# A fused decoder layer on one core: masks, score banks, compressed product and gates of its attention

## The chip, the cores and the metric

One core of a Trainium2 chip runs the whole layer as one program. The time is device microseconds of one execution; the kernel before takes 1240.49 us, the median of three runs (1238.05 to 1242.54). One more execution was profiled, and all rows below come from it.

## The reference, cut to what matters

The layer takes 512 tokens of width 1024. Two token mixers run side by side on the normalised input: a gated linear recurrence (HGRN2, 8 heads) and a sparse attention with 16 query heads in 4 groups, each group sharing one key/value head of width 64. Their outputs are gated, projected, added to the input; a squared-ReLU MLP and a per-layer embedding follow.

The attention has three branches, each a masked softmax, added with per-head gates:

```python
s = einsum('bgrqd,bgnd->bgrqn', qb, k_cmp)                    # compressed keys, 31 of them
p_cmp = masked_softmax(s, cmp_end <= t_pos); o_cmp = p_cmp @ v_cmp
s = einsum('bgrqd,bgqkd->bgrqk', qr, kg)                      # selected blocks
o_sel = masked_softmax(s, key_pos <= t_pos) @ vg
s = einsum('bgrqd,bgkd->bgrqk', qr, kwb)                      # sliding window of 512
o_win = masked_softmax(s, causal and in window) @ vwb
out = gt[0] * o_cmp + gt[1] * o_sel + gt[2] * o_win           # gt: sigmoid gates per head
```

With 512 tokens there are 8 blocks and 16 may be selected, so every earlier block is chosen; the window also covers all of the past. Both the second and the third branch are therefore plain causal softmax attention with keys of their own.

## The kernel before, in words

Values are kept as pairs of fp32r tiles (a rounded high part and the rest as low part), and a product is the sum of two or three matmuls over the pairs. Projections (`job_n`, L125, and `job_t`, L118 with `mm3`, L81) take 256 or 512 columns per matmul. ScalarE casts the high part and VectorE or GpSimd subtracts for the low part (`split`, L59).

The attention part is `attend` (L454), called once per group of four heads. It is a generator that walks over four tiles of 128 queries (t) and two branches (br). For each (t, br), `scores` (L457) handles the group's four heads one after another. A head takes a bank of the score buffer (two banks, tag `sc`), multiplies its query tile with the high and the low keys (L463, L464; the keys seen are nk = 128, 256, 384 or 512 for t = 0 to 3), and adds the causal mask to the last 128 columns as a third matmul, identity times mask, both in bf16 (L465). VectorE takes the row maximum, negated, from the bank (L467); ScalarE computes the exponential from the bank into a tile P and the row sum beside it (L469). After four heads VectorE inverts the sums (L472) and multiplies them with the branch's gates (L474); three of the P tiles are scaled by the result on VectorE (L477), the fourth on ScalarE (L479). The loop starts the scores of the next (t, br) before `values` (L482) of the present one: for each block of 128 keys the four P tiles are transposed (L158) into a bank, split into `pth` (ScalarE) and `ptl` (VectorE), and multiplied with the values into the bank `py` (L489, L490).

The compressed branch is computed for the group beforehand. `cmp_probs` (L440) leaves its weights, already gated, transposed in `chl`: rows 0 to 63 hold the high and low parts of an even tile t, rows 64 to 127 those of the odd tile after it. After branch 1 of a tile, L517 multiplies the tile's 64 rows with the compressed values `vch` (filled in `cmp_out`, L315 to L317, the same values in all four groups of 32 rows) into `py`, and `store` (L492) evacuates it.

The order of instructions in each engine's queue is chosen by a planner that schedules the program by modelled times. Projections of later stages are fillers: `mark` (L67) notes the mask matmuls and some others with weights, and `spread` (L70) ties the starts of projections to these marks, in proportion. GpSimd does the low parts of weights during attention (`lo_eng`), the rotations and small scalings. The tile `vch` and the constant masks are allocated at the start (L213 to L228).

Of the kernel before, what the change touches and what calls it, by code (L numbers as in the profile page):

```python
# [7 lines left out]
FT = mybir.dt.float32  # L8
FR = mybir.dt.float32r
# [19 lines left out]
def hybrid_layer(ctx: ExitStack, tc: tile.TileContext, x, p, w_in, w_branch_a, w_branch_b, w_out,  # L29
# [21 lines left out]

    ident = const.tile([128, 128], FT, name="ident")
    identr = const.tile([128, 128], FR, name="identr")
    identb = const.tile([128, 128], BF, name="identb")
    half = const.tile([128, 4], FT, name="half")
    dve.memset(half, -0.5)

# [110 lines left out]
    with tc.tile_pool(name="pre", reuse_waits="tile", bufs=2) as pre, \  # L168
            tc.tile_pool(name="prep", reuse_waits="tile", bufs=2, space=PSUM) as prep:
        xs = [pre.tile([128, D], FT, name="xt", bufs=4) for _ in range(NT)]  # L170
        wrow = pre.tile([1, D], FT, name="wrow", bufs=1)
        ones = pre.tile([1, 128], FT, name="ones", bufs=1)
        dve.memset(ones, 1.0)
        sp.dma_start(xs[0], x[0:128])
        act.dma_start(wrow, norm_pre_mix)
        act.dma_start(ident, c_ident)
        first_chunks = n_chunks(w_in, [(C_KS, 128), (C_VS, 128)])
        for t in range(1, NT):
            sp.dma_start(xs[t], x[t * 128:(t + 1) * 128])
        act.copy(identr, ident)  # L180
        dve.tensor_copy(identb, ident)
        wps = prep.tile([128, D], FT, name="wps", bufs=1)
        for i in range(2):
            pe.matmul(wps[:, i * 512:i * 512 + 512], ones, wrow[:, i * 512:i * 512 + 512],
                      start=True, stop=True)
        for t in range(NT):
            sq = pre.tile([128, D], FT, name="sq")
            ss = pre.tile([128, 1], FT, name="ss")
            rs = pre.tile([128, 1], FT, name="rs")
            act.activation(sq, xs[t], AF.Square, accum_out=ss)  # L190
            rstd(rs, ss, EPS, pre)
            un = pre.tile([128, D], FT, name="un")
            for g in range(2):
                c = slice(g * 512, g * 512 + 512)
                dve.scalar_tensor_tensor(un[:, c], xs[t][:, c], rs, wps[:, c], op0=OP.mult, op1=OP.mult)
                ps = transpose4(prep, [un[:, (4 * g + i) * 128:(4 * g + i + 1) * 128] for i in range(4)])
                s = (slice(None), slice(4 * g, 4 * g + 4), slice(t * 128, t * 128 + 128))
                split(uh[s], ul[s], ps.rearrange("p (k t) -> p k t", k=4))
# [14 lines left out]
    ns_keep = tc.alloc_tile_pool(name="nsk", reuse_waits="tile", bufs=1, side="right")  # L213
    bd = ns_keep.tile([128, 4, 64], FT, name="bd")
    pool.memset(bd, 0.0)
    vch = ns_keep.tile([128, 4, 128], FR, name="vch")
    gate = ns_keep.tile([128, NT, 48], FT, name="gate")
    cmask = ns_keep.tile([128, NT, 32], FT, name="cmask")
    sp.dma_start(cmask, c_cmask.rearrange("(t p) n -> p t n", p=128))
# [2 lines left out]
    dve.tensor_scalar(valid[:, 0:1], cmask[:, 0, 0:1], 0.0, None, op0=OP.is_equal)  # L222
    rope = ns_keep.tile([128, NT, 32], FT, name="rope")
    sp.dma_start(rope, c_rope.rearrange("(t p) n -> p t n", p=128))
    causal = ns_keep.tile([128, 128], BF, name="causal")
    cf = ns_keep.tile([128, 128], FT, name="cf")
    sp.dma_start(cf, c_causal)
    dve.tensor_copy(causal, cf)  # L228
# [53 lines left out]
    def cmp_out(b, ph):  # L282
# [25 lines left out]
        else:  # L308
# [4 lines left out]
            vc = cp.tile([32, 4, 64], FT, name="vc")  # L313
            act.activation(vc, po[:32, :256].rearrange("p (g d) -> p g d", g=4), AF.Copy, scale=0.5)
            for r in range(0, 128, 32):  # L315
                act.copy(vch[r:r + 32, :, 0:64], vc)
                dve.tensor_sub(vch[r:r + 32, :, 64:128], vc, vch[0:32, :, 0:64])  # L317


    ns = tc.alloc_tile_pool(name="ns", reuse_waits="tile", bufs=2, side="right")  # L320
# [133 lines left out]
    def attend(g, qs, chl, kvs):  # L454
        P2, j = divmod(g, 2)

        def scores(t, br):  # L457
            KH, KL, V = kvs[br]
            q, nk = slice(t * 128, t * 128 + 128), (t + 1) * 128
            Ps, sums = [], at.tile([128, 4], FT, name="sums", bufs=4)  # L460
            for h in range(4):
                ps = nsp.tile([128, 512], FT, name="ps_s", tag="sc")
                pe.matmul(ps[:, :nk], qs[h][:, q], KH[j][:, :nk], start=True, stop=False)  # L463
                pe.matmul(ps[:, :nk], qs[h][:, q], KL[j][:, :nk], start=False, stop=False)  # L464
                mark(pe.matmul(ps[:, nk - 128:nk], identb, causal, start=False, stop=True), nk / 512)  # L465
                nm = at.tile([128, 1], FT, name="nm", bufs=6)
                dve.tensor_reduce(nm, ps[:, :nk], axis=AX.X, op=OP.max, negate=True)  # L467
                pt = at.tile([128, 512], FT, name="P", bufs=8)
                act.activation(pt[:, :nk], ps[:, :nk], AF.Exp, bias=nm, accum_out=sums[:, h:h + 1])  # L469
                Ps.append(pt)  # L470
            r = at.tile([128, 4], FT, name="r", bufs=4)
            dve.reciprocal(r, sums)  # L472
            gi = 16 * (br + 1) + 4 * g
            dve.tensor_mul(r, r, gate[:, t, gi:gi + 4])  # L474
            for h in range(4):
                if h < 3:
                    dve.tensor_scalar(Ps[h][:, :nk], Ps[h][:, :nk], r[:, h:h + 1], None, op0=OP.mult)  # L477
                else:
                    act.activation(Ps[h][:, :nk], Ps[h][:, :nk], AF.Copy, scale=r[:, h:h + 1])  # L479
            return Ps  # L480
# [28 lines left out]
        for i, (t, br) in enumerate(steps):  # L509
# [3 lines left out]
            values(t, br, pend, py)  # L513
            pend = nxt
            if br:
                o = t % 2 * 64
                pe.matmul(py, vch[o:o + 64, g], chl[t // 2][o:o + 64], start=False, stop=True)  # L517
                store(t, py)
            yield True

# [707 lines left out]
```

## Time and profile before

| | |
|---|---|
| median of three runs | 1240.49 us (1238.05 to 1242.54) |
| profiled execution | 1240.57 us, span 1238.8 us from the first to the last instruction |
| TensorE busy | 1195.2 us (96%), 7199 matmuls |
| VectorE, ScalarE, GpSimd busy | 794.4, 629.3, 169.3 us |
| mean granted TensorE clock | 0.996 of full speed |
| attention stage | from about 129 to 411 us |

Times in rows are microseconds unless marked ns. L465 is line 465 of the kernel. PE is TensorE's matmuls, PEld its weight loads, DVE VectorE, ACT ScalarE, POOL GpSimd. [...]

### The profile page before, as it was taken

How to read it: one execution, taken by the hardware profiler on the slowest of the kernel's cores; microseconds unless marked ns; L12 is line 12 of the kernel's file. 1: busy time of each engine (PE TensorE's matmuls, PEld its weight loads, DVE VectorE, ACT ScalarE, POOL GpSimd, SP SyncE). 2: the span in 40 equal slices, each digit the busy share in tenths (PEclk: the TensorE clock that was granted, in tenths of full speed). 3: DMA queues.
4: the chain of work that ended last, by engine and by line, in shares of the span. 5: the costliest groups of instructions: out<-in, count | busy, mean ns of one | idle time of the engine just before them, and what ended most of it. 6: DMA issues, size and time to landing. Idle time of an engine off the chain costs nothing.

```text
span 1238.8 us, 18866 instructions
## 1 busy us (share of the span) xinstructions
PE 1195.2 (96%) x7199; PEld 1029.5 (83%) x7199; DVE 794.4 (64%) x1448; ACT 629.3 (51%) x1273; POOL 169.3 (14%) x281
## 2 busy tenths in 40 slices
PE   7999999999999999999999999997999999999997
PEld 6888877787777889898978778887989889889885
DVE  6775687847787366767685454587527547555664
ACT  6555677756777433434443222465627437336442
POOL 2022332342321110101010110100000000000000
PEclk9999999999999999999999999999999999999999
DMA  6336222212112432222223994533413424226401
GB/s 180 104 107 167 64 54 54 52 52 61 50 40 74 137 102 69 69 69 69 69 69 103 238 232 151 182 132 113 137 49 106 133 68 137 85 69 225 166 18 68
DMA packets 131597, 127.63 MB, mean 103 GB/s; under 512 B 8578, under 2 KB 107826, under 8 KB 131507
## 3 DMA queue, kind: packets, MB, share of 16 engines
q1 hardware_dynamic: 121504, 109.59, 30.2%
q0 software_dynamic: 3200, 10.49, 3.1%
q10 hardware_dynamic: 6802, 6.36, 1.6%
q8 instruction: 56, 0.92, 0.3%
q14 instruction: 35, 0.28, 0.1%
HBM read 111.73 MB, written 14.68 MB: 102 GB/s over the span
## 4 chain that ended last, share of the span: by engine, by line
PE 83%; DVE 7%; DMA 4%; ACT 4%; issue 1%; SPq 0%; POOL 0%; ACTq 0%; DVEq 0%; POOLq 0%
PE up L1033 11%; PE ps L82 7%; PE ps L83 7%; PE ps L84 7%; PE acc L1116 5%; PE acc L1115 5%; PE acc L1117 5%; PE ps L133 5%; PE ps L135 4%; PE ps L134 4%; PE lev L711 3%; PE tr L158 3%; PE acc L915 2%; PE acc L917 2%; PE acc L916 2%; PE tr L1033 2%
## 5 line engine op out<-in xcount | busy, mean ns | idle before, releaser
L60 ACT CAST whi<-raw 128x1024 fp32r<-128x1024 f32 (+1 forms) x199 | 207.4, 1046 | 219.9 <-PE acc L1117 59.1
L61 DVE TENSOR_TENSOR wlo<-raw,whi 128x1024 fp32r<-128x1024 f32 (+1 forms) x181 | 220.8, 1224 | 124.9 <-ACT whi L60 120.1
L133 PE MATMUL ps<-whi,uh 128*128 128x256 f32 (+1 forms) x512 | 148.0, 290 | 1.4 <-DVE kcd L257 0.5
L135 PE MATMUL ps<-whi,ul 128*128 128x256 f32 (+1 forms) x512 | 146.6, 287 | 0.0
L134 PE MATMUL ps<-wlo,uh 128*128 128x256 f32 (+1 forms) x512 | 146.3, 286 | 0.2 <-DVE wlo L61 0.2
L82 PE MATMUL ps<-uh,whi 128*128 128x512 f32 x288 | 118.2, 411 | 0.0
L84 PE MATMUL ps<-uh,wlo 128*128 128x512 f32 x288 | 114.7, 398 | 0.3 <-DVE wlo L61 0.3
L83 PE MATMUL ps<-ul,whi 128*128 128x512 f32 x288 | 114.7, 398 | 0.0
L1116 PE MATMUL acc<-wlo,fh 128*128 128x512 f32 x256 | 101.0, 395 | 0.0
L1115 PE MATMUL acc<-whi,fh 128*128 128x512 f32 x256 | 100.3, 395 | 0.0
L133 PEld LDWEIGHTS ps<-whi,uh 128*128 128x128 f32 x512 | 96.7, 189 | 4.0 <-PE cps L84 0.7
L1117 PE MATMUL acc<-whi,fl 128*128 128x512 f32 x256 | 99.9, 395 | 0.0
L134 PEld LDWEIGHTS ps<-wlo,uh 128*128 128x128 f32 x512 | 96.9, 189 | 1.3 <-DVE wlo L61 0.5
L135 PEld LDWEIGHTS ps<-whi,ul 128*128 128x128 f32 x512 | 96.7, 189 | 0.6 <-issue 0.2
L469 ACT ACTIVATE P<-ps_s,nm 128x128 f32<-128x128 f32 (+3 forms) x128 | 67.7, 530 | 28.3 <-DVE nm L467 25.9
L467 DVE TENSOR_REDUCE nm<-ps_s 128x1 f32<-128x128 f32 (+3 forms) x128 | 61.2, 484 | 26.4 <-PE ps_s L465 25.8
L61 DVE TENSOR_TENSOR ptl<-tr,pth 128x512 fp32r<-128x512 f32 x82 | 55.5, 684 | 26.5 <-ACT pth L60 26.2
L84 PEld LDWEIGHTS ps<-uh,wlo 128*128 128x128 f32 x288 | 54.1, 188 | 12.6 <-DVE wlo L61 0.4
L83 PEld LDWEIGHTS ps<-ul,whi 128*128 128x128 f32 x288 | 54.2, 188 | 10.2
L82 PEld LDWEIGHTS ps<-uh,whi 128*128 128x128 f32 x288 | 54.2, 188 | 10.0
L1033 PE MATMUL up<-mgh,whi 128*128 128x256 f32 x192 | 54.5, 285 | 3.6 <-ACT mgh L60 3.6
L1117 PEld LDWEIGHTS acc<-whi,fl 128*128 128x128 f32 x256 | 48.2, 188 | 11.2
(323 smaller groups left out, 2942.8 us busy)
## 6 DMA issues: line engine op xcount, KB each, us to landing
raw<-in_w_in_dram SPq DMA_DIRECT2D x58, 512.0 KB, 3.8
raw<-in_w_up_dram SPq DMA_DIRECT2D x32, 512.0 KB, 3.8
raw<-in_w_down_dram SPq DMA_DIRECT2D x32, 512.0 KB, 4.0
raw<-in_w_in_dram SPq DMA_DIRECT2D x17, 256.0 KB, 3.5
raw<-in_w_branch_a_dram SPq DMA_DIRECT2D x8, 512.0 KB, 7.9
raw<-in_w_branch_b_dram SPq DMA_DIRECT2D x32, 128.0 KB, 6.4
raw<-in_w_out_dram SPq DMA_DIRECT2D x8, 512.0 KB, 4.8
raw<-in_w_ple_gate_dram SPq DMA_DIRECT2D x8, 512.0 KB, 5.2
```

The lines of the kernel that those rows point to most:

```text
L60: act.copy(hi, src)
L61: (lo_eng or dve).tensor_sub(lo, src, hi)
L82: rec.append(pe.matmul(ps, lh, rh, start=first, stop=False).ins)
L83: pe.matmul(ps, lh, rl, start=False, stop=False)
L84: pe.matmul(ps, ll, rh, start=False, stop=last)
L133: rec.append(pe.matmul(o, stat[0][:, k, s], hi[:, i], start=(k == 0), stop=False).ins)
L134: pe.matmul(o, stat[0][:, k, s], lo[:, i], start=False, stop=False)
L135: pe.matmul(o, stat[1][:, k, s], hi[:, i], start=False, stop=(k == NK - 1))
L1033: pe.matmul(ps[:, c], l[:, k, cs], r[:, k], start=f and n == 0, stop=e and n == 2, skip_group_check=True)
L1115: pe.matmul(ps, fh[:, k % 4, s], hi[:, k % 2], start=(k == 0), stop=False)
L1116: pe.matmul(ps, fh[:, k % 4, s], lo[:, k % 2], start=False, stop=False)
L1117: pe.matmul(ps, fl[:, k % 4, s], hi[:, k % 2], start=False, stop=(k == NK - 1))
```

## The change

The mask and its identity become fp32r, and the bf16 identity goes. In `scores`, as many heads as fit 512 columns share a bank: four at nk = 128, two at 256, one at 384 and 512. The score matmuls of these heads write their own columns of the bank, one mask matmul then covers the last 128 columns of each head (the same mask, repeated), and one maximum over the bank gives a column per head. The exponentials stay one per head. The compressed values get two copies, one with zeros in rows 64 to 127 and one with zeros in rows 0 to 63, and L517 becomes a product over all 128 rows with the copy that fits the tile's parity. The tile is cleared on GpSimd first. The gates are no longer multiplied into the inverted sums of four heads: the scaling of a P tile on VectorE takes the gate as its second scalar, and the fourth head's factor is multiplied by itself, for ScalarE.

```diff
-    identb = const.tile([128, 128], BF, name="identb")
-        dve.tensor_copy(identb, ident)
-    vch = ns_keep.tile([128, 4, 128], FR, name="vch")
+    vch = ns_keep.tile([128, 2, 4, 128], FR, name="vch")
+    pool.memset(vch.bitcast(FT), 0.0)
-    causal = ns_keep.tile([128, 128], BF, name="causal")
+    causal = ns_keep.tile([128, 128], FR, name="causal")
             for r in range(0, 128, 32):
-                act.copy(vch[r:r + 32, :, 0:64], vc)
-                dve.tensor_sub(vch[r:r + 32, :, 64:128], vc, vch[0:32, :, 0:64])
+                o = r // 64
+                act.copy(vch[r:r + 32, o, :, 0:64], vc)
+                dve.tensor_sub(vch[r:r + 32, o, :, 64:128], vc, vch[0:32, 0, :, 0:64])
...
-            for h in range(4):
-                ps = nsp.tile([128, 512], FT, name="ps_s", tag="sc")
-                pe.matmul(ps[:, :nk], qs[h][:, q], KH[j][:, :nk], start=True, stop=False)
-                pe.matmul(ps[:, :nk], qs[h][:, q], KL[j][:, :nk], start=False, stop=False)
-                mark(pe.matmul(ps[:, nk - 128:nk], identb, causal, start=False, stop=True), nk / 512)
-                nm = at.tile([128, 1], FT, name="nm", bufs=6)
-                dve.tensor_reduce(nm, ps[:, :nk], axis=AX.X, op=OP.max, negate=True)
-                pt = at.tile([128, 512], FT, name="P", bufs=8)
-                act.activation(pt[:, :nk], ps[:, :nk], AF.Exp, bias=nm, accum_out=sums[:, h:h + 1])
-                Ps.append(pt)
+            nm = at.tile([128, 4], FT, name="nm", bufs=3)
+
+            n = max(1, 512 // nk)
+            for h0 in range(0, 4, n):
+                bank = nsp.tile([128, 512], FT, name="ps_s", tag="sc")
+                ps = bank[:, :n * nk].rearrange("p (h k) -> p h k", h=n)
+                for i in range(n):
+                    for K in (KH, KL):
+                        pe.matmul(ps[:, i], qs[h0 + i][:, q], K[j][:, :nk], start=(i == 0 and K is KH),
+                                  stop=False, skip_group_check=True)
+                mark(pe.matmul(ps[:, :, nk - 128:nk], identr, causal[:, None, :].to_broadcast([128, n, 128]),
+                               start=False, stop=True, skip_group_check=True), n * nk / 512)
+                dve.tensor_reduce(nm[:, h0:h0 + n], ps, axis=AX.X, op=OP.max, negate=True)
+                for i in range(n):
+                    h = h0 + i
+                    pt = at.tile([128, 512], FT, name="P", bufs=8)
+                    act.activation(pt[:, :nk], ps[:, i], AF.Exp, bias=nm[:, h:h + 1],
+                                   accum_out=sums[:, h:h + 1])
+                    Ps.append(pt)
...
-            dve.tensor_mul(r, r, gate[:, t, gi:gi + 4])
+            gs = gate[:, t, gi:gi + 4]
+            dve.tensor_scalar(r[:, 3:4], r[:, 3:4], gs[:, 3:4], None, op0=OP.mult)
             for h in range(4):
                 if h < 3:
-                    dve.tensor_scalar(Ps[h][:, :nk], Ps[h][:, :nk], r[:, h:h + 1], None, op0=OP.mult)
+                    dve.tensor_scalar(Ps[h][:, :nk], Ps[h][:, :nk], r[:, h:h + 1], gs[:, h:h + 1],
+                                      op0=OP.mult, op1=OP.mult)
...
-                o = t % 2 * 64
-                pe.matmul(py, vch[o:o + 64, g], chl[t // 2][o:o + 64], start=False, stop=True)
+                pe.matmul(py, vch[:, t % 2, g], chl[t // 2], start=False, stop=True)
```

## Rows read from the trace of the kernel before

**Rows 1.** Chain that ended last: share of the span by engine.
```profile
PE 83%; DVE 7%; DMA 4%; ACT 4%; issue 1%; SPq 0%; POOL 0%; ACTq 0%; DVEq 0%; POOLq 0%
```

**Rows 2.** Windows: length, busy PE, PEld, DVE, ACT, POOL, clock, DMA share, GB/s.
```profile
129.00:411.00 282.00, 266.60 (x1709) 213.34 (x1707) 210.52 (x474) 199.79 (x514) 86.78 (x120) 0.99 0.20 53
205.00:209.00 4.00, 2.28 (x13) 1.57 (x13) 3.82 (x13) 2.54 (x10) 2.65 (x3) 0.98 0.23 50
```

**Rows 3.** Waits of PE in attention: who for whom, total us, times, longest.
```profile
PE ps_s L463 <- ACT P L469: 5.8, 12, 0.9
```

**Rows 4.** Waits of PEld in attention, the compressed product's weight loads.
```profile
PEld py L517 <- issue: 4.0, 16, 0.4
```

**Rows 5.** Timeline of PE around one compressed product: start, us, instruction.
```profile
181.39 0.46 PE L490 MATMUL py<-ptl,V 128*128 128x512 f32 x1
181.78 0.50 PE L517 MATMUL py<-chl,vch 64*128 64x512 f32 x1
182.21 0.66 PE L158 MATMUL tr<-ident,P 128*128 128x128 f32 x4
```

**Rows 6.** Timeline of PE, 512-column projections without a wait.
```profile
410.12 0.39 PE L83 MATMUL ps<-ul,whi 128*128 128x512 f32 x1
410.35 0.39 PE L84 MATMUL ps<-uh,wlo 128*128 128x512 f32 x1
```

**Rows 7.** Timeline of PEld, the load of the second matmul of rows 6.
```profile
410.12 0.19 PEld L84 LDWEIGHTS ps<-uh,wlo 128*128 128x128 f32 x1
```

**Rows 8.** Timeline of PE, one head's mask at 256 keys.
```profile
146.66 0.28 PE L464 MATMUL ps_s<-kt,qs 128*128 128x256 f32 x1
146.78 0.23 PE L465 MATMUL ps_s<-causal,identb 128*128 128x128 bf16 x1
...
147.02 0.28 PE L134 MATMUL ps<-wlo,uh 128*128 128x256 f32 x1
```

**Rows 9.** Timeline of PEld, one head at 128 keys and the next.
```profile
129.40 0.19 PEld L463 LDWEIGHTS ps_s<-kt,qs 128*128 128x128 f32 x1
129.52 0.19 PEld L464 LDWEIGHTS ps_s<-kt,qs 128*128 128x128 f32 x1
129.68 0.10 PEld L465 LDWEIGHTS <-identb 128*128 128x128 bf16 x1
129.69 0.20 PEld L463 LDWEIGHTS ps_s<-kt,qs 128*128 128x128 f32 x1
```

**Rows 10.** Lines of DVE in attention, by form: busy us, mean ns, idle before.
```profile
L467 DVE TENSOR_REDUCE nm<-ps_s 128x1 f32<-128x512 f32 x32 | 21.7, 684 | 5.6 <-PE ps_s L465 5.5
...
L467 DVE TENSOR_REDUCE nm<-ps_s 128x1 f32<-128x256 f32 x32 | 13.3, 418 | 7.6 <-PE ps_s L465 7.4
L474 DVE TENSOR_TENSOR r<-r,gate 128x4 f32<-128x4 f32 x32 | 11.8, 368 | 0.6
L477 DVE TENSOR_SCALAR P<-P,r 128x512 f32<-128x512 f32 x24 | 10.5, 489 | 0.2
...
L467 DVE TENSOR_REDUCE nm<-ps_s 128x1 f32<-128x128 f32 x32 | 8.8, 283 | 8.1 <-PE ps_s L465 8.0
```

**Rows 11.** Lines of DVE in the recurrence: a scaling with two scalars.
```profile
L683 DVE TENSOR_SCALAR f<-th,lba,lbb 128x512 f32<-128x512 f32 x8 | 4.3, 541 | 0.0
```

**Rows 12.** Source line 385: a small scaling by a scalar from memory (min/median/max ns).
```profile
L385 DVE TENSOR_SCALAR gate<-gate,valid x4: 220/234/238, 82.8 to 91.4; 128x16 f32<-128x16 f32 x4
```

**Rows 13.** Timeline of DVE, one gate product.
```profile
134.47 0.77 DVE L474 TENSOR_TENSOR r<-r,gate 128x4 f32<-128x4 f32 x1
```

**Rows 14.** Timeline of POOL at the same time.
```profile
132.85 2.37 POOL L61 TENSOR_TENSOR wlo<-raw,whi 128x1024 fp32r<-128x1024 f32 x1 [1.80 <-ACT whi L60]
```

**Rows 15.** Timeline of POOL at the start of the program.
```profile
0.74 0.31 POOL L215 MEMSET bd<- 128x256 f32 x1 [0.29 <-POOLq L1217]
6.10 0.54 POOL L153 TENSOR_TENSOR rs<-ms,half 128x1 f32<-128x1 f32 x1 [5.05 <-DVE ms L152]
```

**Rows 16.** Lines of PE in attention: first score matmul of 256 keys, idle before.
```profile
L463 PE MATMUL ps_s<-kt,qs 128*128 128x256 f32 x32 | 11.5, 361 | 2.9 <-ACT P L469 2.8
```

## The prediction

> **What bounds the kernel now.** I read the chain of waits first: TensorE carries 83% of it, VectorE 7%, ScalarE 4% [rows 1]. So the time is TensorE's queue unless a stage says otherwise. Then the attention stage, from 129 to 411 us, cut out by windows: TensorE busy 266.6 of 282 us, VectorE 210.5, ScalarE 199.8 [rows 2]. The reader is to see two things: TensorE has 15 us without work there, and in a few pockets the roles turn round (205 to 209: VectorE 3.82 of 4 us, TensorE 2.28). After 411 us nothing is touched, so whatever attention ends earlier should arrive at the end. In the waits, TensorE stands at the first score matmul for a score bank that the exponentials hold: 5.8 us in 12 waits [rows 3]. Last, the queue itself in order of time. Busy durations overlap there, so I price by the distance from one start to the next: 0.23 us for a 512-column matmul [rows 6].
>
> **The product with the compressed values.** Sixteen of them, each on 64 rows. The distances around one: 0.39 us from the matmul before it to the product, 0.43 us from the product to the next [rows 5]; before its weight load that unit pauses, put down to issue: 4.0 us in sixteen times, 0.25 each [rows 4]. Two 512-column matmuls on all rows take 2 x 0.23 = 0.46. Over 128 rows, with a zero half in the weights, the same 512 columns stream, so each should save 0.82 - 0.46 = 0.36, sixteen of them 5.8 us. Bounds: 5.8 gone, or nothing, if the pause belongs to something else than the half-height operand. I take 5.8, since the pause sits on all sixteen. [...]
>
> **The mask matmul, by length of the keys.** There are 32 heads of each length. At 256 keys the second score matmul starts at 146.66, the mask at 146.78, and the second matmul after that at 147.02: 0.36, where two steps without a mask are 0.24, so a bf16 mask costs 0.12 [rows 8]. 32 masks x 0.12 = 3.8; now 16 of 256 columns at the same 0.12 = 1.9. Gain 1.9 us. At 128 keys one head takes 0.29 between its first load and the next head's, four 1.16 [rows 9]; now 8 loads x 0.12 and one 512-column mask at 0.23 are 1.19. That is 0.03 in each of 8 calls: nothing. At 384 and 512 keys 64 masks stay single and turn from bf16 to fp32r weights. An fp32 load takes 0.19 against 0.10 [rows 9], but it starts one matmul early, under a score matmul of 384 or 512 columns. Bounds: -0.01 x 64 = -0.6 us (what the rounding of the rows leaves), or the whole difference exposed, 0.09 x 64 = +5.8. The nearest row is the step of 0.12 between two fp32 loads of 128-column matmuls [rows 9], equal to what the bf16 mask costs: I take 0. [...]
>
> TensorE's own work so falls by 5.8 + 1.9 = 7.7 us (with the bounds: 8.3 at best; -3.9, a loss, with no gain at the product and every fp32 load exposed). Only where TensorE is the link does it count; the chain says 83% [rows 1]: 6.4 us.
>
> **VectorE.** Maxima: 32 x 0.283 become 8 of 512 elements at 0.684 (9.1 to 5.5), and 32 x 0.418 become 16 x 0.684 (13.4 to 10.9): -6.1 us [rows 10]. The scaling of P reads a second scalar: two-scalar instructions of 512 take 0.541 where the one-scalar form takes 0.489 [rows 10, 11]; 96 x 0.052 = +5.0. The gate product on 4 columns becomes one of 1 column, 0.234 by the nearest small one with a scalar from memory [rows 12] against 0.16 undisturbed: 32 x 0.07 = +2.3. Sum +1.2 us. The mean of the gate product is 0.368 because some stand still: one took 0.77, from 134.47 to 135.24, and GpSimd's 2.37 us subtraction ended at 135.22 [rows 10, 13, 14]. The stalls' sum is 32 x (0.368 - 0.16) = 6.6 us. The one-column form may escape, but the scaling of P behind it works between the same memories, so I let the stall move there: 0; if it went, -6.6. At VectorE's 7% of the chain, +1.2 is +0.1 on the end.
>
> **What waits move.** A shared bank lets TensorE issue the scores of two or four heads without waiting for an exponential in between; the 5.8 us are the most that can go. Against it the first exponential starts later: with four heads by (1.19 - 0.29) for the matmuls and (0.684 - 0.283) for the maximum, 1.3 us, in 8 calls; with two by 0.24 + 0.27 = 0.5 us, in 8 calls. Queued behind it on ScalarE are the casts of the transposed P; TensorE's value matmuls wait for those. That is 14.5 us in all, covered wherever filler projections stand in TensorE's queue, and they do in most of the stage. In pockets like 205 to 209 they don't. I choose one call in five as uncovered, 2.9 us, the pockets being short beside the stage, and half of the bank waits as gone, 2.9: zero together.
>
> **Small edits at nothing.** Clearing the doubled value tile on GpSimd: four times the columns of the tile cleared before it in 0.31 us, 1.2 us at about 0.7, while GpSimd's next work starts at 6.10 after 5.05 idle [rows 15]; if that cover were gone the first normalisation would slip 1.2 us. Dropping the bf16 identity frees one short VectorE copy. The product of an even tile now waits for the odd tile's rows of the compressed weights too; these are written in a run of four, ahead of the products, and at worst it waits one subtraction of 512 columns, 0.68 [rows 10], per group.
>
> Forecast: 1240.57 (profiled) - 6.4 + 0.1 = 1234.3; the median of the runs is 0.08 lower: **1234**.
>
> **Rivals.** (1) *The waits go too.* Bank waits of 5.8 vanish and all 7.7 count: 1227. For it: 2.8 of them stand before heads of 256 keys [rows 16]. Against: VectorE is full in exactly these pockets, so the next wait is at P. [...] (3) *Slower: bank-wide maxima hold the exponentials back.* One place, the start of each call at 128 and 256 keys; price up to 14.5, less 6.4: 1248.6. It decides once more than 6.4 of 14.5 is uncovered, that is fewer fillers around than before. For it: the pockets with VectorE full; fillers are tied to mask matmuls, and a call now has one or two of these where it had four, so they can bunch. The order in each queue is written anew by the planner from its own modelled times, so the trace of before cannot say where fillers will stand. Against: TensorE has work in 266.6 of 282 us [rows 2].
>
> **How the numbers follow.** Forecast 0.50 (1231 to 1237 alone), rival 1 0.16, rival 2 0.22, rival 3 0.12. 0.3% is 3.7 us, about what can be told from no change here. Below 1236.8: 0.47 + 0.16 + 0.01 = 0.64; within: 0.24; above 1244.2: 0.12. The range 1227 to 1242 leaves out rival 3 and about half of rival 1's faster side.
>
> **What would show it.** Product: distance to its neighbours 0.23 each, no pause before its load; if 0.4 stays, the step is wrong. [...] VectorE: 88 maxima in place of 128 (8 + 16 + 64), those over several heads near 0.68; P scaling at 0.54 for 512. Waits: TensorE for banks under 5.8. The attention stage should end 6 us before 411; an end that comes earlier while the whole doesn't would sink the argument that the rest follows.

## The result and the profile after

The changed kernel takes 1247.44 us (median of 4 runs, 1246.33 to 1249.19) against 1241.3 us beside it: ratio 1.0051, 95% interval [1.0036, 1.0067], that is 6.3 us slower (4.5 to 8.3). The forecast was 1234, the range ended at 1242. All readings of the profile after are from an execution of 1246.33 us with a span of 1244.5; the one of before had 1238.8.

The chain that ended last, in the changed kernel, to be held against [rows 1]:

```profile
PE 69%; DVE 4%; ACT 2%; DMA 1%; issue 1%; SPq 0%; POOL 0%; ACTq 0%; DVEq 0%; POOLq 0%
```

The shares sum to 77%, so this chain could not be followed all the way back; it tells only that TensorE is still the link in the part that was followed. Then windows of the changed kernel: the first stretch of [rows 2], and one from 125 to 425 us that takes in the whole attention stage (columns as there).

```profile
129.00:411.00 282.00, 257.21 (x1635) 220.40 (x1634) 206.47 (x430) 194.60 (x509) 87.76 (x120) 0.97 0.20 53
...
125.00:425.00 300.00, 274.61 (x1758) 235.60 (x1756) 214.11 (x442) 203.02 (x527) 91.53 (x128) 0.97 0.21 57
```

The same long window in the kernel before:

```profile
125.00:425.00 300.00, 284.22 (x1851) 230.15 (x1849) 217.39 (x484) 207.91 (x530) 90.55 (x128) 0.99 0.23 62
```

TensorE idles 25.4 us there instead of 15.8, and its mean granted clock is 0.97 instead of 0.99. TensorE, VectorE and ScalarE are busy 9.6, 3.3 and 4.9 us less in the window; GpSimd is busy 1.0 us more, and the weight loads, which run beside matmuls (0.19 us from 142.79 under a matmul of 142.69 to 143.19, below), 5.5 us. So the time went into waiting and into a slower clock, not into new work of the engine that is the link. The last product with the compressed values starts at 417.72 us, in the kernel before at 411.35: 6.4 us later, where the prediction wanted the stage to end 6 us earlier. So the whole loss arises in this stage and is passed on to the end. Where in it, five-microsecond windows of the changed kernel show best:

```profile
255.00:260.00 5.00, 5.00 (x45) 5.00 (x44) 1.04 (x3) 2.04 (x6) 2.36 (x8) 1.00 0.00 0
260.00:265.00 5.00, 2.18 (x15) 1.64 (x14) 2.77 (x2) 2.44 (x5) 4.19 (x5) 0.94 0.13 25
265.00:270.00 5.00, 2.85 (x10) 2.35 (x11) 0.91 (x2) 0.81 (x2) 1.56 (x2) 0.50 0.65 188
...
280.00:285.00 5.00, 1.97 (x11) 1.20 (x9) 5.00 (x8) 2.47 (x7) 2.45 (x1) 0.99 0.28 76
285.00:290.00 5.00, 5.00 (x19) 4.51 (x19) 3.68 (x10) 2.68 (x9) 0.00 (x0) 0.50 0.27 81
```

and the same ones of the kernel before:

```profile
260.00:265.00 5.00, 4.01 (x24) 2.92 (x22) 3.72 (x5) 2.93 (x6) 5.00 (x6) 1.00 0.37 104
265.00:270.00 5.00, 4.75 (x26) 3.50 (x26) 2.36 (x5) 1.29 (x4) 0.24 (x1) 1.00 0.40 105
280.00:285.00 5.00, 3.44 (x26) 2.63 (x24) 4.59 (x16) 3.82 (x14) 0.59 (x1) 1.00 0.43 109
285.00:290.00 5.00, 4.62 (x32) 3.27 (x32) 4.87 (x11) 4.00 (x12) 0.46 (x1) 1.00 0.00 0
```

Read the second and the last column but two together. After a pause (2.18 and 1.97 of 5 us busy) the granted clock stands at 0.50, the lower of the two levels in the traces of both kernels (the other is 1.00), for 6.8 us from 264.4 and again from 284.9, and a window that is fully busy then passes 19 matmuls, where 32 passed before in a busy time of 4.62 (not the same matmuls, so the counts are only a hint). So each of these two pauses is paid twice. The waits of TensorE from 129 to 411 us in the changed kernel name whom it stood for (total us, times, longest); the two at L339 are in the windows at 260 to 270, and two of those at L157, 2.4 us, in the one at 280:

```profile
PE tr L157 <- DVE P L487: 6.2, 7, 2.0
...
PE ps_s L469 <- ACT P L477: 5.5, 10, 1.4
PE trr L339 <- DVE stage L390: 5.0, 2, 3.6
```

What VectorE was doing meanwhile is seen in the timeline at 280 us (start, us, instruction; the first row holds three scalings, one after the other):

```profile
280.54 2.88 DVE L487 TENSOR_SCALAR P<-P,r,gate 128x128 f32<-128x128 f32 x3
280.62 2.45 POOL L60 TENSOR_TENSOR wlo<-raw,whi 128x1024 fp32r<-128x1024 f32 x1 [14.06 <-ACT whi L59]
283.21 0.33 PE L157 MATMUL tr<-ident,P 128*128 128x128 f32 x1 [1.95 <-DVE P L487]
```

One of the three scalings takes 2.37 us, where their median is 0.34, and ends 0.09 us after GpSimd's subtraction. TensorE's transpose waits 1.95 us for it. The table behind the experiments counts such waits in every run.

The direct effects came as forecast or nearly so. TensorE around one compressed product (L527), and its weight loads:

```profile
142.69 0.50 PE L501 MATMUL py<-ptl,V 128*128 128x512 f32 x1
143.02 0.40 PE L527 MATMUL py<-chl,vch 128*128 128x512 f32 x1
143.26 0.60 PE L157 MATMUL tr<-ident,P 128*128 128x128 f32 x4
```

```profile
142.79 0.19 PEld L527 LDWEIGHTS py<-chl,vch 128*128 128x128 f32 x1
```

0.33 and 0.24 us in place of 0.39 and 0.43 [rows 5]; over the sixteen the medians are 0.233 and 0.235. The pause before the load [rows 4] is gone: it starts 0.10 after the preceding matmul does. VectorE's groups by form, against [rows 10]:

```profile
L487 DVE TENSOR_SCALAR P<-P,r,gate 128x512 f32<-128x512 f32 x24 | 14.6, 660 | 0.0
...
L473 DVE TENSOR_REDUCE nm<-ps_s 128x2 f32<-128x512 f32 x16 | 10.8, 678 | 1.5 <-PE ps_s L471 1.4
L487 DVE TENSOR_SCALAR P<-P,r,gate 128x128 f32<-128x128 f32 x24 | 8.8, 422 | 0.0
L484 DVE TENSOR_SCALAR r<-r,gate 128x1 f32<-128x1 f32 x32 | 6.7, 208 | 0.8
...
L473 DVE TENSOR_REDUCE nm<-ps_s 128x4 f32<-128x512 f32 x8 | 5.4, 688 | 5.9 <-PE ps_s L471 5.8
```

The bank-wide maxima take what was forecast (0.678 and 0.688). The scaling of 512 columns has a mean of 0.660, but that holds two instructions which stood beside GpSimd (2.65 and 1.27 us); its median is the forecast 0.541. The gate product takes less than in the kernel before (6.7 us against 11.8). The waits for a score bank, of which half was to go, stayed: 5.5 us after 5.8 [rows 3].

One more reading set the experiments. TensorE's queue around the preparation of head group 2, cut from the two instruction streams (F projections, a attention instructions, equal neighbours counted once; R transposes of staged tiles, Q the query copies' transposes, C compressed scores):

```
before: F48 a1 F51 a3 R a7 R F3 R F3 a4 R F6 a4 R F3 a4 Q F3 a8 Q F3 a4 C a39
after:  a1 F99 R F3 R F3 a3 R F6 a1 R F3 a1 Q F3 a2 Q F3 C a18
```

Before, attention work of group 1 stood between the links of the chain that prepares group 2; after, most of it had been used up ahead of the chain.

### The profile page after: what moved, and what is told of

Read it like the earlier page. It is cut to its first block, busy times and chain, and to the rows that moved or that the text cites. A ratio compares the mean times of both kernels' runs of the same rounds, so it can differ in the third digit from the quotient of the medians.

```text
span 1244.5 us, 18738 instructions
## 1 busy us (share of the span) xinstructions
PE 1191.8 (96%) x7159; PEld 1040.8 (84%) x7159; DVE 792.9 (64%) x1407; ACT 626.9 (50%) x1273; POOL 170.8 (14%) x282
## 4 chain that ended last, share of the span: by engine, by line
PE 69%; DVE 4%; ACT 2%; DMA 1%; issue 1%; SPq 0%; POOL 0%; ACTq 0%; DVEq 0%; POOLq 0%
PE up L1043 11%; PE ps L81 6%; PE ps L82 6%; PE ps L83 6%; PE acc L1126 5%; PE acc L1125 5%; PE acc L1127 5%; PE lev L721 3%; PE ps L132 3%; PE ps L134 3%; PE ps L133 3%; PE acc L925 2%; PE acc L927 2%; PE acc L926 2%; PE tr L157 2%; PE tr L1043 2%
## 5 line engine op out<-in xcount | busy, mean ns | idle before, releaser
L60 DVE TENSOR_TENSOR wlo<-raw,whi 128x1024 fp32r<-128x1024 f32 (+1 forms) x181 | 220.6, 1223 | 122.2 <-ACT whi L59 121.5
L60 DVE TENSOR_TENSOR ptl<-tr,pth 128x512 fp32r<-128x512 f32 x82 | 55.2, 682 | 21.4 <-ACT pth L59 21.2
L473 DVE TENSOR_REDUCE nm<-ps_s 128x1 f32<-128x384 f32 (+3 forms) x88 | 55.3, 633 | 19.4 <-PE ps_s L471 19.1
L469 PE MATMUL ps_s<-kt,qs 128*128 128x128 f32 (+3 forms) x256 | 62.0, 348 | 5.8 <-ACT P L477 5.5
L59 ACT CAST pth<-tr 128x512 fp32r<-128x512 f32 x82 | 47.2, 589 | 24.4 <-PE tr L157 23.8
```

The costliest lines, as they stand in the source:

```text
L59: act.copy(hi, src)
L60: (lo_eng or dve).tensor_sub(lo, src, hi)
```

## The experiments

The theories. **1**: the loss is the planner's new order of the queues. **2**: the fp32r mask or the longer scaling costs directly. **3**: waiting for a whole shared bank costs. **4**, formed later: GpSimd's long subtractions inside the rotary chain. All times are compared with the kernel before, run beside them on the same chip; "+5" is the ratio less one, times 1241. The tool is a set of ties, added after the last instruction, that gives each queue a stored order; it adds no semaphore and no operation (shortened):

```diff
+    for e, steps in stored_order.items():      # one list for each of the five queues
+        for ins in steps:
+            tc.add_manual_dep(ins, last.name, ...NoSync...)   # behind the one ahead of it
```

In such a kernel the lines stand some 50 to 75 lower. "Held" means tied to the order of the kernel before, "planned" ordered anew. In e5, e11 and all runs from e13 on the ties of `spread` are left out; the stored order takes their place.

**e1, the tie alone**, kernel before, held.

> The kernel before, with nothing changed but that every engine's queue is tied to the order it had. All theories: the same time as before, within 0.3%; the tie by itself costs nothing. Were it slower, the other runs with the held order would have to be read against this one.

1241.32, ratio 0.9995 [0.998, 1.001]. The tie costs nothing that can be told.

**e2, the product over 128 rows alone, held**; diff: the hunks on `vch` and L517.

> The product over 128 rows alone, in the queue order of the kernel before. If the product's price of 16 x 0.36 us is right and TensorE is the link: 5 to 6 us faster than before, 1235.5. If the edit itself is dear (the longer clearing, the wait for the odd tile's rows): the same or slower.

1238.08, 0.9973 [0.9962, 0.9985]: -3.4 us, less gain than expected.

**e3, product, fp32r mask for each head and gates, held**; no shared banks.

```diff
-    mark(pe.matmul(ps[:, nk - 128:nk], identb, causal, start=False, stop=True), nk / 512)
+    mark(pe.matmul(ps[:, nk - 128:nk], identr, causal, start=False, stop=True), nk / 512)
```

> Product over 128 rows, fp32r mask per head and gates as second scalar, each head still with a bank of its own, in the queue order of the kernel before. Theory 1 (the loss is the new order of the queues, the edits are sound): 5 to 7 us faster than before, 1234 to 1236. Theory 2 (the fp32r mask and the second scalar cost more than the product saves): slower than before, up to 1247.

1236.74, 0.996 [0.9945, 0.9974]: -5.0 us. Theory 2 falls: with every fp32r mask and every second scalar in it, the kernel is faster. It beats both kernels.

**e4, the same three edits, planned.**

> The same three edits without shared banks, but the planner orders the queues anew. Theory 1: the order decides, so this one may stand anywhere from 1234 to 1250, and its attention stage shows a stretch of projections alone if it is slow. Theory 3 (the loss is in the shared banks, late exponentials): as fast as with the held order, 1234 to 1236.

1248.63, 1.0058 [1.0041, 1.0074]: +7.2. The same operations differ by 12.2 us with their order, and the loss is there without any shared bank.

**e5, all four edits, held** (a bank's maximum and exponentials at the place of its last head's).

> All four edits, shared banks included, every queue in the order of the kernel before (a shared bank's maximum and exponentials at the place of the bank's last head). Theory 1, the loss is the new queue order alone: 1234 to 1239 us, near the 1236.7 of the three edits in held order, with the 64-value state ahead of the long run of projections as before. Theory 3, waiting for a whole bank costs by itself: 1241 us or more, with idle time of TensorE in front of score matmuls and transposes that the three held edits don't show.

1244.15, 1.0019 [1.0009, 1.0029]: +2.4, 7.4 above e3. Not what theory 1 alone expects: in this order shared banks cost. Two windows of e5, then of e3:

```profile
135.00:140.00 5.00, 2.58 (x11) 1.84 (x9) 2.84 (x8) 3.91 (x17) 3.24 (x6) 0.71 0.42 105
140.00:145.00 5.00, 4.03 (x19) 3.82 (x19) 4.08 (x12) 2.73 (x13) 0.75 (x1) 0.50 0.39 105
```

```profile
135.00:140.00 5.00, 4.21 (x29) 3.44 (x28) 4.05 (x14) 4.09 (x17) 3.67 (x6) 1.00 0.41 105
140.00:145.00 5.00, 4.35 (x29) 3.78 (x29) 4.96 (x16) 4.19 (x13) 0.00 (x0) 1.00 0.40 108
```

The first calls, where four heads share a bank, leave TensorE idle for 2.4 us, and the clock is at 0.50 behind it; the first output tile leaves its bank 4.2 us later than in e3 (153.44 against 149.24).

**e6, one attention step later.** Changed kernel, planned.

```diff
-    advance(a0, 3, a1, 6)
+    advance(a0, 3, a1, 5)
...
-    advance(a1, 4, a2, 7)
+    advance(a1, 5, a2, 7)
```

> The changed kernel, its queues ordered by the planner, but head group 1 gives one attention step less before the preparation of group 2 and one more after it (6 and 4 become 5 and 5). By the queue order made, the run of 99 projection matmuls then comes after 64 value matmuls instead of 71, as in the kernel before, so attention work is left for the chain that prepares group 2's queries. Theory 1 with its place there: 1235 to 1241 us, TensorE busy at least 45 of the 50 us from 250 to 300. If the order costs its time in many places: 1244 us or more.

1252.31, 1.009 [1.0075, 1.0105]: a clear miss. The pause at 260 grew, and another stands ahead of it at 240, where the changed kernel was busy 3.43 of 5 us; two windows of e6:

```profile
240.00:245.00 5.00, 0.91 (x4) 0.54 (x4) 1.89 (x4) 1.51 (x3) 4.35 (x4) 0.74 0.82 217
...
260.00:265.00 5.00, 0.31 (x2) 0.14 (x1) 1.80 (x3) 1.03 (x3) 4.69 (x6) 0.78 0.38 105
```

**e7, the product alone, planned.**

> The product over 128 rows alone, ordered by the planner (held to the old order it gave 1238.1). Its queue order has the 99 projection matmuls in one piece after 65 value matmuls; before they come as 48 and 51 with four transposes between, after 64. Theory 1: this small edit alone shifts the order and loses, 1244 to 1249 us. If the loss needs several edits together: 1237 to 1240 us.

1246.43, 1.0043 [1.0027, 1.0059]: +5.3, against -3.4 held. An edit that makes sixteen matmuls shorter costs 8.7 us by the order that it brings.

**e8, the fp32r mask alone, planned.**

> The fp32r mask for each head alone, ordered by the planner. Its queue order keeps the 48 and 51 projection matmuls after 64 value matmuls, as before. Theory 1 with its place there: 1238 to 1242 us. If any new plan loses, or the fp32r mask does: 1244 us or more.

1241.41, 1.0002 [0.9992, 1.0011]. The mask's weights, in a plan of their own, cost nothing that can be told; this plan keeps the old pattern around group 2. It is no small plan: by the traces 535 of 7199 places on TensorE hold an instruction of another kind than before (636 in e13, below), but only 5 of 281 on GpSimd (19 in e13).

**e9 and e10, attention work kept behind the projections**, changed kernel, planned, with one tie.

```diff
+    behind.append(rec[-1])                      # last projection ahead of spread(1) after q_main(2)
...
+    if behind and kt == 0 and t == 3 and br == 0:      # e10: t == 2 and br == 1
+        tc.add_manual_dep(first, behind.pop().name, ...NoSync...)   # first value matmul
```

> The changed kernel with one more tie and the planner for the rest: the value matmuls of head group 1's last query tile (t=3, first branch, and so all behind them) stay behind the last projection matmul of the run that prepares group 2, so that 64 value matmuls are done ahead of the 99 projections instead of 71, as in the kernel before, and the rest of TensorE's order is unchanged. Theory 1 with its place at 250 to 300 us: 1241 to 1246 us, TensorE busy 42 us or more in that stretch (40.3 in the changed kernel). If the place doesn't matter: 1246 to 1249 us.

> The same tie one step earlier (query tile t=2, second branch), so that about 58 value matmuls are done ahead of the 99 projections and 22 of group 1 are left behind them. Theory 1 with its place at 250 to 300 us: 1238 to 1244 us, less than with the tie at t=3. If the place doesn't matter: 1246 to 1249 us.

1247.53, 1.0054 [1.0032, 1.0075], and 1246.78, 1.0046 [1.0029, 1.0063]: no gain that can be told. TensorE is busier from 250 to 300 us (43.3 and 44.6 against 40.3), but as much is lost elsewhere: the rows of e10 show the pause now at 240.

```profile
240.00:245.00 5.00, 1.62 (x7) 0.88 (x7) 1.81 (x6) 0.84 (x3) 3.15 (x5) 0.68 0.59 143
245.00:250.00 5.00, 4.66 (x29) 4.47 (x30) 0.70 (x2) 0.95 (x2) 0.00 (x0) 0.64 0.20 70
```

That the loss has one place, the stretch from 250 to 300, is refuted. That the cover left for two chains (keys and values, then queries) is too little wherever it is put would explain it; this is not shown.

**e11, all four edits, held, bank early**: as e5, with a bank's scores, mask and maximum at the place of its first head's.

> All four edits in the order of the kernel before, as in the run that gave 1244.2, but a shared bank's scores, mask and maximum stand together at the place of its first head's and each head's exponential at its own old place (the first call of each group as in that run). If the held shared banks lost only by scores spread out ahead of a late maximum: 1232 to 1238 us, at or below the 1236.7 of the three edits without them. If waiting for a whole bank costs by itself, wherever it stands: 1241 to 1246 us.

1240.99, 1.0 [0.9988, 1.0012]: 2.4 us better than e5, still 5.0 above e3.

**e12, the gates alone, held.**

> The gates as second scalar alone, in the order of the kernel before. The product and the fp32r mask and the gates gave -4.8 us together in that order and the product alone -3.4. Theory 1: 1240 to 1242.5 us, the second scalar's 0.05 us each hidden. Theory 2, the longer scaling is on the path: 1244 us or more.

1238.92, 0.9982 [0.9973, 0.9992]: -2.2 us, better than either theory. Its VectorE rows:

```profile
L551 DVE TENSOR_SCALAR P<-P,r,gate 128x512 f32<-128x512 f32 x24 | 11.7, 541 | 0.0
L551 DVE TENSOR_SCALAR P<-P,r,gate 128x256 f32<-128x256 f32 x24 | 11.2, 520 | 0.0
L551 DVE TENSOR_SCALAR P<-P,r,gate 128x384 f32<-128x384 f32 x24 | 10.0, 473 | 0.0
L551 DVE TENSOR_SCALAR P<-P,r,gate 128x128 f32<-128x128 f32 x24 | 7.4, 361 | 0.0
...
L548 DVE TENSOR_SCALAR r<-r,gate 128x1 f32<-128x1 f32 x32 | 6.7, 209 | 0.6
```

The scaling takes 40.3 us against 32.9 in the kernel before (10.5, 8.6, 8.5 and 5.3), +7.4; the gate product 6.7 against 11.8, -5.1. The means mix two things. By medians the second scalar adds 0.057, 0.054, 0.057 and 0.060 us at 128, 256, 384 and 512 columns (0.279 to 0.337, 0.353 to 0.407, 0.415 to 0.472, 0.482 to 0.542), 5.5 us over the 96; the rest are scalings that stood beside GpSimd, up to 1.41 us long at 256 columns.

**e13, the kernel before in the order planned for the product**, not one operation changed.

> The kernel before, not one operation changed, with its five queues in the order that the planner made for the product alone (789 of 6947 places differ on TensorE, 180 of 1448 on VectorE, 170 of 1142 on ScalarE, 22 of 277 on GpSimd). Theory 1, the order is the loss: 1247 to 1251 us, the 8.3 us between the planned and the held product on top of before's 1241. If an order only loses together with the edit's new durations: 1240 to 1244 us.

1250.24, 1.006 [1.0041, 1.0078]: +7.4. The order alone, without any edit, costs as much as the change does. Four windows of e13 and then of e1, which runs the same operations:

```profile
265.00:270.00 5.00, 2.94 (x10) 1.76 (x10) 2.43 (x5) 0.85 (x3) 3.23 (x5) 0.81 0.51 131
270.00:275.00 5.00, 5.00 (x20) 4.16 (x19) 0.98 (x2) 1.04 (x3) 0.00 (x0) 0.50 0.26 79
330.00:335.00 5.00, 2.77 (x12) 1.66 (x12) 4.88 (x6) 2.49 (x7) 2.84 (x3) 0.80 0.67 172
335.00:340.00 5.00, 5.00 (x18) 3.50 (x17) 2.48 (x6) 2.22 (x7) 0.00 (x0) 0.52 0.11 40
```

```profile
265.00:270.00 5.00, 4.76 (x26) 3.51 (x27) 2.44 (x5) 1.29 (x4) 0.29 (x2) 1.00 0.41 107
270.00:275.00 5.00, 5.00 (x36) 4.28 (x35) 1.92 (x7) 3.02 (x10) 0.00 (x0) 1.00 0.00 0
330.00:335.00 5.00, 5.00 (x27) 3.46 (x26) 4.81 (x11) 3.42 (x9) 0.00 (x0) 1.00 0.00 0
335.00:340.00 5.00, 5.00 (x33) 3.96 (x33) 2.10 (x4) 3.43 (x9) 1.93 (x2) 1.00 0.12 28
```

What stands in e13's window at 330, VectorE, GpSimd and TensorE:

```profile
329.50 3.17 DVE L548 TENSOR_SCALAR P<-P,r 128x384 f32<-128x384 f32 x3
329.98 2.47 POOL L115 TENSOR_TENSOR wlo<-raw,whi 128x1024 fp32r<-128x1024 f32 x1
332.72 0.48 PE L229 MATMUL tr<-ident,P 128*128 128x128 f32 x2 [1.46 <-DVE P L548]
```

Again one scaling takes 2.51 us instead of 0.42, until 0.22 us after GpSimd's subtraction has ended, and TensorE waits for it.

**e14, the three edits, only TensorE's queue held.**

> Product, fp32r mask for each head and gates, with TensorE's queue alone held in the order of before; the planner orders the other four (107 of 1448 places differ from before on VectorE, 59 of 1142 on ScalarE). All five held gave 1236.7, all five planned 1248.6. If TensorE's order carries the loss: 1235 to 1239 us. If the others' order does: 1243 to 1249 us.

1242.68, 1.0009 [0.9997, 1.0021]: +1.1, between the held (-5.0) and the planned (+7.2). Neither expectation. The other queues are not those of e4: by the traces GpSimd and the DMA queue stand as in e3, and 89 of 1448 places on VectorE and 72 of 1273 on ScalarE differ from it. So the order of these two alone is worth 6.1 us here; how e4's 12.2 us divide among its queues the run doesn't tell.

**e15, pairs**: as e11, at most two heads in a bank.

```diff
-            n = max(1, 512 // nk)
+            n = min(2, max(1, 512 // nk))
```

> As the held run that gave 1241.0 (all four edits, a bank's scores, mask and maximum at its first head's place), but at most two heads share a bank, so at 128 keys two banks hold two heads each instead of one holding four. If the 4.3 us that sharing lost there (against 1236.7) come from waiting for four heads at the start of a group: 1236 to 1238.5 us. If sharing costs at 256 keys as well: 1239 to 1242 us.

1238.04, 0.9971 [0.9955, 0.9986]: -3.6, 3.6 below e11 and within the uncertainty of e3. So it is the bank of four at 128 keys that costs in the held order; pairs cost nothing that can be told, and bring nothing.

**e16 and e17, GpSimd's order.** The changed kernel in its own planned order, but for five places on GpSimd where a weight-split subtraction (L60) stood ahead of the last addition of a rotary step (L331). The trace of the changed kernel, GpSimd, then VectorE and TensorE:

```profile
263.95 2.33 POOL L60 TENSOR_TENSOR wlo<-raw,whi 128x1024 fp32r<-128x1024 f32 x1
266.25 0.31 POOL L331 TENSOR_TENSOR ra<-ra,rb 128x64 f32<-128x64 f32 x1
```

```profile
266.87 0.22 DVE L390 TENSOR_TENSOR stage<-ra,stage 128x64 fp32r<-128x64 f32 x1 [3.20 <-ACT stage L388]
```

```profile
267.15 0.37 PE L339 MATMUL trr<-identr,stage 128*128 128x128 f32 x1 [3.55 <-DVE stage L390]
```

> The changed kernel with all queues held in the order that the planner made for it, but for five swaps on GpSimd: the last addition of a rotary step (L331, 0.31 us) comes ahead of the 2.35 us subtraction of a weight split (L60) that stands directly before it. The trace of the changed kernel has it at 263.95 to 266.28, then the addition, then TensorE's transpose after 3.55 us of waiting and a granted clock of 0.50. Theory 4, the planner's order costs by GpSimd's long subtractions inside these chains: 1240 to 1244 us, TensorE's wait for the staged tile under 2 us in all. If these waits are covered by others behind them: 1246 to 1249 us.

> As the run before, but the whole last rotary step (L328 to L331) comes ahead of both weight-split subtractions around it, in the same five places. Theory 4: 1238 to 1243 us, not above the run with the five swaps. If the first subtraction is needed sooner than the rotary step, TensorE waits for the split weights in its place: above the run with the swaps.

1249.2, 1.0073 [1.0058, 1.0089], and 1251.48, 1.0093 [1.0078, 1.0108], against 1.0051 [1.0036, 1.0067] for the changed kernel: no gain in e16, and a loss in e17. The rows of e16 say why:

```profile
265.14 0.32 POOL L401 TENSOR_TENSOR ra<-ra,rb 128x64 f32<-128x64 f32 x1
265.42 2.34 POOL L113 TENSOR_TENSOR wlo<-raw,whi 128x1024 fp32r<-128x1024 f32 x1
```

```profile
265.77 2.07 DVE L460 TENSOR_TENSOR stage<-ra,stage 128x64 fp32r<-128x64 f32 x1 [1.02 <-ACT stage L458]
```

```profile
267.89 0.37 PE L409 MATMUL trr<-identr,stage 128*128 128x128 f32 x1 [3.22 <-DVE stage L460]
```

The addition came out of the subtraction's way, but VectorE's next link, a subtraction of 64 columns that takes 0.22 us undisturbed, now stood for 2.07, until GpSimd's ended. TensorE waited 3.22 instead of 3.55. The subtraction hits the chain from either side, so the swap doesn't take its cost away, and theory 4 is refuted only in that moving the addition is no cure. TensorE's waits for VectorE instructions that stood beside GpSimd even grew, from 5.7 us in the changed kernel to 10.6 (e16) and 12.0 (e17).

**e18, the order of e13 with the same swap in its three places.**

> The kernel before, no operation changed, in the order planned for the product alone (1250.2 us), with the same swap in the three places where that order has it (before's own order has two). Theory 4: 1246 to 1249 us. If GpSimd's order isn't what costs there: 1249 to 1251 us.

1246.17, 1.0051 [1.0034, 1.0068], against 1.006 [1.0041, 1.0078] without it: 1.1 us apart by the ratios (4 by the medians, on two chips), and the intervals overlap, so no effect can be told.

**The sum, in one table.** From each profiled execution: the span; TensorE's idle time from 125 to 425 us; the clock that was not granted there (sixty windows of 5 us, 5 x (1 - granted clock) each, summed); what is left of the span. An estimate, since the clock is also low in some idle time (in the changed kernel it is at 0.50 from 264.4 us, and TensorE idle until 267.15). The last column is a part of the idle time: TensorE's waits for a VectorE instruction that lasted over 0.3 us more than the median of its line and form.

```
                              span    idle   clock   rest    behind VectorE
before                       1238.8   15.8    1.7   1221.3    0.0
e1  before, held             1237.8   15.1    3.4   1219.3    0.0
e13 before, new order        1252.4   18.6   13.7   1220.1    3.7
e2  product, held            1234.5   17.0    1.7   1215.8    0.0
e7  product, planned         1243.1   19.5   11.9   1211.7    3.5
e3  three edits, held        1234.1   15.4    5.1   1213.6    0.0
e14 three, TensorE held      1240.8   20.2    6.8   1213.8    0.4
e4  three edits, planned     1246.2   20.8   10.2   1215.2    3.9
e15 four edits, pairs, held  1237.0   18.2    5.1   1213.7    0.0
e11 four edits, held, early  1239.1   21.0    5.1   1213.0    0.0
e5  four edits, held         1242.7   23.2   10.3   1209.2    1.7
after                        1244.5   25.4    8.5   1210.6    5.7
```

The rest is lower than before by 5.5 to 12.1 us in every row with edits, whatever the order, and by 1.2 and 2.0 in the two without: of the size that the prediction gave the edits' own work (7.7). Idle time and clock undo it: +16.4 us in the changed kernel. Between e1 and e13, with equal work, the order adds 3.5 us of idle time and 10.3 us of clock. That is one execution each, e13's (1254.15 us) a long one of its kernel, and the clock of the kernel before (mean 0.996) is at the upper end of its executions (0.987 to 0.997). By the mean clock of every execution, span x (1 - clock), an estimate, is 15.4 us in e13 (6 executions), 9.2 in e1 (10), 14.0 in the changed kernel (4) and 9.0 in the kernel before (15): 6.2 of 9.1 us between the mean times of e13 and e1.

The last column is what these pauses have in common; it is read from the traces alone, and no run tests it. In all kept traces, every VectorE instruction from 125 to 425 us that ran over 0.3 us past its median overlapped one on GpSimd and ended within 0.3 us of its end. VectorE loses much the same time in this way in either order: 18.0 us in 15 instructions in the kernel before, 19.1 in 17 in e13, 16.2 in 12 in the changed kernel. But in the orders held to the kernel before TensorE waits directly for none of them, or one (e5), and in all planned orders that lose it waits 3.5 to 12.0 us for them. From e1 to e13 this is all of the added idle time, from e2 to e7 too, from e3 to e4 3.9 of 5.4. In e8, which loses nothing, it is 0.8.

## Why the prediction was wrong

**The step that failed** is that the sum has no term for the new order of the queues. The part on what waits move called the delays of the new chains "covered wherever filler projections stand in TensorE's queue, and they do in most of the stage", with one call in five uncovered. That took the cover of the old queue for the new one, and the clock behind a pause stood in no term. The text knew that the order is written anew, but used it only as an argument for rival 3, at 0.12. The runs put the new order at +8.0 us with no edit at all (e13 against e1), +8.7 with the product (e7 against e2) and +12.2 with three edits (e4 against e3), more than all gains together.

**A second term was too small**: the waits that the shared banks move, at zero (2.9 us uncovered less 2.9 of bank waits gone). Held, they cost 5.0 us (e11 against e3) to 7.4 (e5 against e3). Half of the bank waits did go there (5.9 us in e3, 2.5 in e11), but TensorE's waits for a scaled P, ahead of the transposes, rose from 2.3 us to 8.0. In the changed kernel not even the bank waits went (5.5).

**Rival 3** gave 1248.6, near the 1247.4 measured, but its mechanism is only part of it, so the nearness is in the main luck. Bank-wide maxima do hold the start of a group back (e5, e11), and the bank of four is what costs there (e15). In the planner's order, though, shared banks make no difference that can be told: 1.0051 with them, 1.0058 without (e4), and the loss is whole without them.

**The product**: mechanism right, 0.82 us of queue became 0.47, sixteen times 0.35 = 5.6 us against 5.8 forecast. At the end -3.4 [-4.7, -1.9] arrived (e2), where 83% would have been 4.8. The load of the full-height product runs beside a matmul on all rows: a 128-row load starts at 142.79 under a 128-row matmul of 142.69 to 143.19, as one did at 410.12 in the kernel before [rows 6, 7].

**The mask**: 0 for the single fp32r masks was right; e8 excludes the bound of +5.8, every fp32 load exposed, and with it rival 2, whose chance of 0.22 was put on that. The held runs say the same without a new plan: the product (-3.4) and the gates (-2.2) alone add up to -5.6, with the mask they gave -5.0. One more thing shows in e8: in the kernel before, the bf16 mask's loads paused 14.1 us in 65 times, put down to issue like those at the product [rows 4]; in e8 these pauses are gone, as in the changed kernel (none before its 88 mask loads), and nothing is gained. Such a pause alone was no price here. The 1.9 us at 256 keys was not measured apart.

**VectorE**: the second scalar was right (5.5 us by medians against 5.0), the term that was mis-sized is the stalls beside GpSimd, put at 0. In the held order (e12) those of the gate product go, the longest of the one-column form being 0.218 us, and they do not come back in full at the scaling: the terms of the gates, +7.3 in the forecast (5.0 and 2.3), come to +2.3 (7.4 less 5.1). In the changed kernel's order they do come back: scalings stand 7.9 us beside GpSimd, where in the kernel before it was 6.7 at the gate product and 1.0 at the scaling. And the end moved by -2.2 [-3.4, -1.0] in e12, where 7% of +7.3 made +0.5. ScalarE's waits for the gate product fell from 8.6 to 3.3 us, so a shorter link between the exponentials and the transposes would explain it; this was not tested by itself.

**Small edits**: nothing of them shows.

**The reading of the profile** that misled: "after 411 us nothing is touched, so whatever attention ends earlier should arrive" is true, but the stage's 15 us without work were taken as given. They are what the order makes of the stage: another order makes 18.6 of the same operations (e13), and the changed kernel has 25.4.

**What stays open**: why the planner's new orders are worse, by a rule that could be mended. Moving one step (e6), keeping work behind (e9, e10) and moving GpSimd's additions (e16, e17) each moved the pauses and won nothing. The traces point at one thing that all losing orders share, TensorE waiting behind VectorE instructions that stand beside GpSimd; taking the long subtractions off GpSimd in a losing order would test it, and no run did. It is not the whole: e14 loses 6.1 us against e3 with 0.4 us of such waits.

## What to carry to other kernels

Where something orders the queues anew from modelled durations, an edit has two effects, its own and that of the new order; here the second was two to three times the first, and of the other sign. Hold the old order while an edit is judged: the three edits that looked 7 us bad were 5 us good, and that version (1236.74) is the one to keep. In a forecast, give the new order a spread of its own as soon as one duration changes (here from nothing, e8, to 12 us, e4), and price a pause of TensorE above its length, for the clock behind it (0.50 for 6.8 us, twice, in the changed kernel). When VectorE seems slow, compare means with medians first: the difference may be another engine (0.660 against 0.541 at the scaling of 512 columns here).

## What the runs showed of the hardware

- Some pauses of TensorE were followed by the lower clock. In e5 it was busy 2.58 of 5 us from 135, in no pause longer than 1.78 us, and the next 5 us had 0.50; e3, busy 4.21 there, kept 1.00. Not every pause was: e1, busy 3.22 of 5 us from 325, kept 1.00. Over all executions of the two the clock is some 6.2 of the 9.1 us between e13 and e1 (an estimate, above).
- A VectorE subtraction of 64 columns that reads two tiles took 0.22 us alone and 2.07 beside GpSimd's 2.34 us subtraction, ending 0.08 us after it (e16). What the two share, no run shows.
- The scaling of P, which reads one tile and scalars for each row, stands in the same way: 2.37 us instead of 0.34 at 128 columns (changed kernel, 280.79 us). The product of one column by a scalar never did, in 32 instructions of e12 (0.192 to 0.218 us), where 8 of the 32 products of two 4-column tiles did in the kernel before (up to 1.65 us).
- A second per-partition scalar makes the scaling slower by 0.054 to 0.060 us at 128, 256, 384 and 512 columns alike (medians of e12 against those of the kernel before).
